# Second feed-forward product in one pass per column block: eleven groups in place of three lots, the last group in eight products

## The chip, the cores and the metric

The kernel runs on one core of one Trainium2 chip. The metric is the device time of one launch in microseconds (us). TensorE (PE) multiplies, VectorE (DVE) and ScalarE (ACT) work on tiles, GpSimd (POOL) and SyncE (SP) issue most of the transfers (DMAs).

## The reference

One encoder layer on x of 512 x 2048 (all float32): a root-mean-square norm, a wide input projection, an mLSTM in both directions and differential attention, two branch projections with gates, an output projection with residual, and then a gated feed-forward block and a last norm. The change is in the feed-forward block:

```python
h2 = _rmsnorm(x, norm2_w[l])
gate, up = jnp.split(h2 @ w_ffn_in[l], 2, axis=-1)     # D_FF = 5632
x = x + (jax.nn.silu(gate) * up) @ w_ffn_out[l]        # 5632 x 2048
...
return _rmsnorm(x, final_norm_w)
```

## The kernel before, in words

Every float32 product is made of three matmuls: each operand is split into a high part (a cast on ScalarE, L151) and a low part (a subtraction on VectorE, L152), and `mm3` (L145) adds high x high, low x high and high x low in PSUM.

The output projection (`wo_chunk`), the first feed-forward product (`fi_chunk`) and the second (`fo_chunk`) go through `seven` (L310), a Winograd form of Strassen's scheme: a group is 512 rows of the inner dimension, cut into 2 x 2 blocks, and seven block products (Q1 to Q7) take the place of eight. A column block is 1024 columns wide, two halves of 512. For all groups of a call the body runs three passes: Q1, Q5 and Q6 of every group; then Q2, Q3 and Q7 (the last group in another order); then Q4. Each product is 12 matmuls of 128 x 512 on the banks a, b or c (two PSUM tiles each). After the last group of a product, `post` evicts or adds the bank.

- *Right factors.* Per group six raw blocks a to f of 128 x 1024 (512 KB) come from memory by SP (`load`, L194), into 6 tiles `raw`. `t1_make` to `t4_make` form the sums on VectorE (t2 lives from the first pass to the third), and `parts` splits each of the seven factors into `whi` and `wlo`, three tiles each. `take` keeps two pieces ahead of the product, `issue` loads six raw blocks ahead.
- *Left factors.* For the second product they are the gated activations. The seven forms X11, S1, S2, X12, S3, S4, X22 of a group (128 x 512, 256 KB each) were written to memory by `turned` at the end of each `fi_chunk`. `loaded` (L438) brings them back by DMAs on POOL, and `factor` splits each into a high and a low tile, in the narrow tiles `x_` (32 of 128 x 512) or `t_` (39).
- *Lots.* All eleven groups' split factors do not fit in SBUF at once, so L834 cuts them into lots of 4, 4 and 3 groups. `lot_forms` loads and splits a lot's 28 (or 21) factors; it is called at Q2 of the chunk before, and its steps run one after each product through the list `behind` (`work`, L301). Each lot is used for both column blocks n = 0, 1: six chunks in all, in the order (lot 0, n 0), (lot 0, n 1), (lot 1, n 0) and so on.
- *Ends of chunks.* `added` (L649) evicts the banks. In lots 0 and 1 the eight output tiles of a chunk are added to `x1d` in memory by adding stores on POOL (L667). In the last lot the residual is fetched from `x1d` and added in SBUF, and `final` (L845) squares, scales and stores the rows.

Operations that are due later stand in a list with a program clock (`later`, `tick`). A scheduler then orders each engine's queue; within a queue everything runs in order.

## Time and profile before

| what | value |
|---|---|
| median of 3 runs | 2753.08 us (2750.37 to 2759.2) |
| the profiled execution's own time | 2750.09 us |
| its span, first to last instruction | 2748.3 us |
| mean granted TensorE clock | 0.988 |
| busy: PE, DVE, ACT, POOL | 2665.9, 1883.0, 1186.9, 194.3 us |
| moved by DMA | 435.59 MB, mean 158 GB/s |

Busy time is a sum over stages with different limits. PEclk is the share of full speed at which TensorE's clock was granted in a stretch. A DMA share of 1 means that all 16 transfer engines were busy. A matmul's shown length holds its pipeline; the distance between the starts of two is what it costs. In the rows, fi is the first feed-forward product, fo the second, fs a left factor on its way to fo, wo the output projection, and a name's L number is a line of the kernel.

### The profile page before, as it was taken

The numbers are of one execution on the slowest core, as the hardware profiler recorded it, in microseconds if no ns is written. First come the engines' busy times: TensorE is split into PE (matmuls) and PEld (weight loads), VectorE is DVE, ScalarE is ACT, GpSimd is POOL, SyncE is SP. The second block draws the span as 40 slices with busy tenths as digits, with TensorE's granted clock in tenths as the row PEclk, the third lists the DMA queues.
The fourth block names the chain that finished last, engine by engine and source line by source line (L and its number), as shares of the span: only waits on it lengthen the run. The fifth ranks groups of instructions, "written<-read, shape, count | busy, mean of one in ns | idle before, by whom it ended". The sixth has DMA issues, their size and how long they took to land.

```text
span 2748.3 us, 33249 instructions
## 1 busy us (share of the span) xinstructions
PE 2665.9 (97%) x12736; PEld 2227.7 (81%) x12736; DVE 1883.0 (69%) x2403; ACT 1186.9 (43%) x1641; POOL 194.3 (7%) x309
## 2 busy tenths in 40 slices
PE   7999999999999999999999999999999999898997
PEld 6888888888888888887778888888888878677776
DVE  5677776333444442487788888878888889686876
ACT  5444443222344432245464444444444455453544
POOL 2110100000000000001110000000000010111211
PEclk9999999999999999999999999999999999999999
DMA  5433332333322222347765555565555576677665
GB/s 194 125 105 95 81 104 97 111 112 111 100 92 93 92 92 92 127 151 215 242 193 185 189 176 180 175 208 188 182 184 191 197 253 194 213 214 214 209 201 162
DMA packets 138736, 435.59 MB, mean 158 GB/s; under 512 B 17848, under 2 KB 18408, under 8 KB 138576
## 3 DMA queue, kind: packets, MB, share of 16 engines
q1 hardware_dynamic: 103680, 353.56, 38.3%
q0 software_dynamic: 25056, 63.38, 9.1%
q10 hardware_dynamic: 9840, 16.52, 1.9%
q8 instruction: 100, 1.64, 0.2%
q14 instruction: 60, 0.49, 0.1%
HBM read 378.06 MB, written 44.84 MB: 154 GB/s over the span
## 4 chain that ended last, share of the span: by engine, by line
PE 61%; DVE 12%; issue 12%; DMA 11%; POOL 1%; ACT 1%; SPq 0%; ACTq 0%; DVEq 0%; POOLq 0%
PE fi_b L147 8%; PE ga_b L147 6%; PE gm_b L147 6%; PE aqk_b L147 6%; PE fi_a L147 6%; PE fi_c L147 6%; PE mqk_b L147 3%; PE mo_b L147 3%; PE ba_b L147 3%; PE mv_p L147 3%; DVE wlo_fi_Q L152 3%; PE av_p L147 3%; PE bm_b L147 2%; DVE wlo_fo_Q L152 2%; DMA raw_fo_b<-in_w_ffo 2%
## 5 line engine op out<-in xcount | busy, mean ns | idle before, releaser
L151 ACT CAST whi_fi_Q<-fi_Q_t 128x1024 fp32r<-128x1024 f32 x88 | 92.6, 1052 | 117.5 <-PE fi_b L147 95.5
L147 PE MATMUL aqk_b<-xh,whi_aqk 128*128 128x512 f32 x256 | 102.6, 404 | 11.9 <-ACT whi_aqk L151 7.8
L152 DVE TENSOR_TENSOR wlo_fi_Q<-fi_Q_t,whi_fi_Q 128x1024 fp32r<-128x1024 f32 x88 | 106.3, 1219 | 2.4 <-ACT whi_fi_Q L151 2.4
L147 PE MATMUL aqk_b<-xl,whi_aqk 128*128 128x512 f32 x256 | 102.2, 399 | 1.0 <-DVE xl L551 1.0
L333 DVE TENSOR_TENSOR raw_fi_e<-raw_fi_e,raw_fi_f 128x1024 f32<-128x1024 f32 x44 | 53.9, 1225 | 70.7 <-DMA raw_fi_e<-in_w_ffi 70.4
L147 PE MATMUL aqk_b<-xh,wlo_aqk 128*128 128x512 f32 x256 | 101.9, 398 | 0.3 <-DVE wlo_aqk L152 0.3
L147 PE MATMUL ga_b<-xh,whi_ga 128*128 128x512 f32 x256 | 100.0, 390 | 0.0
L147 PE MATMUL gm_b<-xh,whi_gm 128*128 128x512 f32 x256 | 99.7, 389 | 0.0
L147 PE MATMUL ga_b<-xl,whi_ga 128*128 128x512 f32 x256 | 99.7, 389 | 0.0
L147 PE MATMUL ga_b<-xh,wlo_ga 128*128 128x512 f32 x256 | 99.6, 389 | 0.0
L147 PE MATMUL gm_b<-xl,whi_gm 128*128 128x512 f32 x256 | 99.6, 389 | 0.0
L147 PE MATMUL gm_b<-xh,wlo_gm 128*128 128x512 f32 x256 | 99.6, 389 | 0.0
L152 DVE TENSOR_TENSOR wlo_gm<-raw_gm,whi_gm 128x1024 fp32r<-128x1024 f32 x32 | 39.2, 1225 | 84.4 <-ACT whi_gm L151 84.3
L320 DVE TENSOR_TENSOR raw_fi_b<-raw_fi_b,raw_fi_a 128x1024 f32<-128x1024 f32 x44 | 53.9, 1224 | 50.9 <-DMA raw_fi_b<-in_w_ffi 48.3
L151 ACT CAST whi_ga<-raw_ga 128x1024 fp32r<-128x1024 f32 x32 | 33.7, 1053 | 115.1 <-PE ga_b L147 62.4
L152 DVE TENSOR_TENSOR wlo_ga<-raw_ga,whi_ga 128x1024 fp32r<-128x1024 f32 x32 | 39.1, 1223 | 57.2 <-ACT whi_ga L151 57.2
L151 ACT CAST whi_gm<-raw_gm 128x1024 fp32r<-128x1024 f32 x32 | 33.7, 1053 | 103.1 <-PE gm_b L147 70.6
L151 ACT CAST whi_fi_Q<-raw_fi_e 128x1024 fp32r<-128x1024 f32 x44 | 46.4, 1055 | 70.7 <-PE fi_b L147 49.9
L151 ACT CAST whi_fi_Q<-raw_fi_b 128x1024 fp32r<-128x1024 f32 x44 | 46.6, 1058 | 67.0 <-PE fi_c L147 51.1
L151 ACT CAST whi_fi_Q<-raw_fi_f 128x1024 fp32r<-128x1024 f32 x44 | 46.5, 1056 | 64.1 <-PE fi_c L147 61.5
L147 PE MATMUL av_p<-whi_av,xh 128*128 128x256 f32 x256 | 72.9, 285 | 0.8 <-ACT whi_av L151 0.8
L147 PE MATMUL mv_p<-whi_mv,xh 128*128 128x256 f32 (+1 forms) x256 | 73.6, 287 | 0.0
(541 smaller groups left out, 8841.8 us busy)
## 6 DMA issues: line engine op xcount, KB each, us to landing
raw_fi_a<-in_w_ffi SPq DMA_DIRECT2D x44, 512.0 KB, 3.9
raw_fi_b<-in_w_ffi SPq DMA_DIRECT2D x44, 512.0 KB, 4.5
raw_fi_c<-in_w_ffi SPq DMA_DIRECT2D x44, 512.0 KB, 4.5
raw_fi_d<-in_w_ffi SPq DMA_DIRECT2D x44, 512.0 KB, 4.4
raw_fi_f<-in_w_ffi SPq DMA_DIRECT2D x44, 512.0 KB, 4.2
raw_fi_e<-in_w_ffi SPq DMA_DIRECT2D x44, 512.0 KB, 4.4
raw_ga<-in_w_ga SPq DMA_DIRECT2D x32, 512.0 KB, 3.5
raw_gm<-in_w_gm SPq DMA_DIRECT2D x32, 512.0 KB, 3.5
```

Source lines behind the costliest of these rows:

```text
L147: T.matmul(dst, lhs[l], rhs[r], start=first and i == 0, stop=last and i == 2, skip_group_check=skip)
L151: A.copy(hi, src)
L152: V.tensor_tensor(lo, src, hi.bitcast(F32), ALU.subtract)
L320: V.tensor_tensor(raws[r12], raws[r12], raws[r11], ALU.add)
L333: V.tensor_tensor(raws[r12], raws[r12], raws[r22], ALU.add)
```

## The change

- One pass per column block: `fo_chunk(n)` runs all groups, twice in all in place of six chunks. The adding stores to `x1d` go; the residual is fetched once per column block.
- No left factor stays. `stream()` lists, for both column blocks, every form in the order in which the products need it (74 per column block). Each is fetched four steps ahead by POOL, split where it is due, one step after each product, and kept until its product has used it. So each of them is loaded and split twice.
- The first ten groups use the seven products; the eleventh is computed plainly with eight (W12, W22, W11, W21, each times two left blocks), between the second and the third pass, on a fourth pair of banks d. Its forms S1 to S4 are not formed.
- `x_` becomes 16 tiles of 128 x 1024, which hold the high and the low part of one factor. In the second product these tiles take t2 and every second raw block, and eight raw blocks are loaded ahead instead of six.
- In `added`, the end of a tile whose residual is fetched by DMA is put 8000 ns of the program clock later, for the output projection too; the transposes behind it come 2000 after the end in all cases.

```diff
-    xpool = ctx.enter_context(tc.tile_pool(name="xpool", bufs=32))
+    xpool = ctx.enter_context(tc.tile_pool(name="xpool", bufs=16))
...
-        return xpool.tile([P, 512], dt, tag="x", name=name)
+        return xpool.tile([P, 1024], dt, tag="x", name=name)
...
-            name, src = sources[len(raws)]
-            raw = wpool.tile([P, src.shape[-1]], F32, tag="raw", name=f"raw_{name}", bufs=6)
+            name, src, x = sources[len(raws)]
+            raw = (x_(f"raw_{name}") if x else
+                   wpool.tile([P, src.shape[-1]], F32, tag="raw", name=f"raw_{name}", bufs=6))
...
-            load(need + 6)
+            load(need + (8 if sources[need][2] is not None else 6))
...
-    def seven(name, src, order, forms, post, start=None):
+    def seven(name, src, order, forms, post, start=None, plain=None, spare=False):
...
-            return source(f"{name}_{n}{g}", src(g, half, lot))
+            return source(f"{name}_{n}{g}", src(g, half, lot),
+                          len(sources) % 2 == 1 if spare else None)
...
-                t2[g] = ppool.tile([P, 1024], F32, tag="p", name=f"{nm}_t2")
+                t2[g] = (x_(f"{nm}_t2") if spare else
+                         ppool.tile([P, 1024], F32, tag="p", name=f"{nm}_t2"))
...
+        if plain is not None:
+            for n, at, to, posts in (
+                    ("W12", (0, 1), [("c", "X11"), ("d", "X21")], []),
+                    ("W22", (1, 1), [("c", "X12"), ("d", "X22")], ["D", "Q3"]),
+                    ("W11", (0, 0), [("a", "X11"), ("b", "X21")], []),
+                    ("W21", (1, 0), [("a", "X12"), ("b", "X22")], ["Q2"])):
+                r = raw(plain, *at, n)
+                add(n, plain, r, held(lambda r=r: raws[r]), to, posts)
...
+                for b_, f_ in to:
+                    if b_ not in bank:
+                        bank[b_] = [ps(f"{nm}_{b_}{i}") for i in range(2)]
+                    while f_ not in forms(g):
+                        work(True)
+                    hi, lo = forms(g)[f_]
...
+                    if b_ != to[-1][0]:
+                        work()
...
-    def factor(name, g, n, out, f_, src):
-        w = [slots(g, n + i)(f"{name}_{f_}{'hl'[i]}", F32R).rearrange("p (k c) -> p k c", k=2)
-             for i in range(2)]
+    def factor(name, n, out, f_, src):
+
+        if n < 16:
+            w = x_(f"{name}_{f_}", F32R)
+            w = [w[:, :512], w[:, 512:]]
+        else:
+            w = [t_(f"{name}_{f_}{i}", F32R) for i in "hl"]
+        w = tuple(x.rearrange("p (k c) -> p k c", k=2) for x in w)
         split(src, *w)
...
-            if final:
-                final(t, c, x[q, i])
-            else:
-                G.dma_start(x1d[t][c], x[q, i], accum_op=ALU.add)
+            final(t, c, x[q, i])
...
-                    end(22, i)
+                        later(8000, lambda i=i: end(22, i))
+                elif q_ == "D":
+                    V.tensor_tensor(x[22, i], x[22, i], bank["d"][i], ALU.add)
+                    fetch(22, i)
+                    later(8000, lambda i=i: end(22, i))
                 elif q_ == "Q3":
                     V.tensor_tensor(x[12, i], x[12, i], c_[i], ALU.add)
-                    if final:
-                        fetch(12, i)
-                    end(12, i)
+                    fetch(12, i)
+                    later(8000, lambda i=i: end(12, i))
...
-                later(9000 if c % 2 else 2000, lambda: turned(f"h2{c}", pair, 0, h2X[c], i,
+                later(2000, lambda: turned(f"h2{c}", pair, 0, h2X[c], i,
...
-            if q_ == "Q2" and j == NFB - 1:
-                lot_forms(0)
+            if q_ == "Q4" and j == NFB - 1:
+                stream()
...
-    LOTS = [range(0, 4), range(4, 8), range(8, NFB)]
+    GR = range(NFB - 1)
+
+    def stream():
+        need = [(g, f_) for g in GR for f_ in ("X11", "S1", "S2")]
+        need += [(g, f_) for g in GR[:-1] for f_ in ("X12", "S4", "S3")]
+        need += [(GR[-1], f_) for f_ in ("S3", "S4", "X12")]
+        need += [(NFB - 1, f_) for f_ in ("X11", "X21", "X12", "X22")]
+        need += [(g, "X22") for g in GR]
+        need = [(n, *gf) for n in range(2) for gf in need]
+        got = {}
+
+        def fetch(n):
+            if n < len(need):
+                _, g, f_ = need[n]
+                got[n] = half(f"fs{g}_{f_}")
+                G.dma_start(got[n], fgd[g][f_].rearrange("p (k c) -> p k c", k=2))
+
+        def make(n):
+            fetch(n + 4)
+            m, g, f_ = need[n]
+            factor(f"fs{m}_{g}", 16, fgf[m, g], f_, got.pop(n))
+
+        for n in range(4):
+            fetch(n)
+        for m, g, _ in need:
+            fgf[m, g] = {}
+        when(lambda: True, [lambda n=n: make(n) for n in range(len(need))])
...
-        seven(f"fo{m}_{n}", lambda g, h_, l: a["w_ffo"][n, g, h_, l], lot, lambda g: fgf[g],
-              added(f"fo{m}_{n}", n, *((lambda t, c: x1d[t][c], final) if last else ())), start)
+        seven(f"fo{n}", lambda g, h_, l: a["w_ffo"][n, g, h_, l], GR, lambda g: fgf[n, g],
+              added(f"fo{n}", n, lambda t, c: x1d[t][c], final, True), start, NFB - 1, True)
...
-    for m in range(len(LOTS)):
-        for n in range(2):
-            fo_chunk(m, n)
+    for n in range(2):
+        fo_chunk(n)
```

The first place is POOL's queue. Before, at the end of the first chunk (lot 0, n 0), where the last loads of lot 0 are followed by that chunk's adding stores:

```order
L446 DMA fs3_S4_18681<-fg3_S4d_157 128x512
L446 DMA fs3_X22_18683<-fg3_X22d_158 128x512
L667 DMA x1d2_1_109<-fo0_0_x220_18801 128x512
L667 DMA x1d3_1_113<-fo0_0_x221_18807 128x512
L667 DMA x1d0_1_101<-fo0_0_x120_18803 128x512
L667 DMA x1d1_1_105<-fo0_0_x121_18809 128x512
L667 DMA x1d0_0_100<-fo0_0_x110_19093 128x512
L667 DMA x1d1_0_104<-fo0_0_x111_19096 128x512
L667 DMA x1d2_0_108<-fo0_0_x210_18805 128x512
L667 DMA x1d3_0_112<-fo0_0_x211_18811 128x512
L446 DMA fs4_X11_19422<-fg4_X11d_159 128x512
```

In the changed kernel, where the first column block goes from its first pass to the second:

```order
L867 DMA fs9_S1_18950<-fg9_S1d_196 128x512
L867 DMA fs9_S2_18976<-fg9_S2d_195 128x512
L867 DMA fs0_X12_19000<-fg0_X12d_134 128x512
L867 DMA fs0_S4_19025<-fg0_S4d_136 128x512
L867 DMA fs0_S3_19051<-fg0_S3d_135 128x512
L867 DMA fs1_X12_19075<-fg1_X12d_141 128x512
L867 DMA fs1_S4_19100<-fg1_S4d_143 128x512
L681 DMA fo0_x210_19130<-x1d2_0_108 128x512
L867 DMA fs1_S3_19140<-fg1_S3d_142 128x512
L681 DMA fo0_x211_19137<-x1d3_0_112 128x512
```

The eight adding stores in a row are gone; loads of single factors follow one another in the order of use, with residual fetches (fo0_x) between them.

The second place is VectorE's queue. Before, in the second chunk (lot 0, n 1), second pass, where the factors of lot 1 (fs4 to fs7) are split beside the chunk's own weights:

```order
L152 TENSOR_TENSOR wlo_fo0_1_Q72_19580<-raw_fo0_1_e2_19428,whi_fo0_1_Q72_19579 128x1024
L152 TENSOR_TENSOR fs6_S1l_19627<-fs6_S1_19523,fs6_S1h_19626 128x512
L152 TENSOR_TENSOR fs7_X11l_19682<-fs7_X11_19595,fs7_X11h_19681 128x512
L152 TENSOR_TENSOR fs4_X12l_19760<-fs4_X12_19673,fs4_X12h_19759 128x512
L152 TENSOR_TENSOR wlo_fo0_1_Q73_19611<-raw_fo0_1_e3_19480,whi_fo0_1_Q73_19610 128x1024
L152 TENSOR_TENSOR fs7_S1l_19706<-fs7_S1_19597,fs7_S1h_19705 128x512
L152 TENSOR_TENSOR fs4_S3l_19780<-fs4_S3_19675,fs4_S3h_19779 128x512
L152 TENSOR_TENSOR wlo_fo0_1_Q33_19631<-raw_fo0_1_f3_19457,whi_fo0_1_Q33_19630 128x1024
```

In the changed kernel, first column block, first pass, groups 3 to 5:

```order
L152 TENSOR_TENSOR wlo_fo0_Q53_18635<-raw_fo0_b3_18415,whi_fo0_Q53_18634 128x1024
L152 TENSOR_TENSOR fs0_4_X11l_18653<-fs4_X11_18550,fs0_4_X11h_18652 128x512
L331 TENSOR_TENSOR fo0_Q66_t2_18883<-raw_fo0_b6_18656,raw_fo0_c6_18682 128x1024
L152 TENSOR_TENSOR wlo_fo0_Q63_18661<-fo0_Q63_t2_18658,whi_fo0_Q63_18660 128x1024
L152 TENSOR_TENSOR fs0_4_S1l_18679<-fs4_S1_18575,fs0_4_S1h_18678 128x512
L152 TENSOR_TENSOR wlo_fo0_Q14_18685<-raw_fo0_a4_18465,whi_fo0_Q14_18684 128x1024
L152 TENSOR_TENSOR fs0_4_S2l_18703<-fs4_S2_18601,fs0_4_S2h_18702 128x512
L323 TENSOR_TENSOR raw_fo0_b7_18731<-raw_fo0_b7_18731,raw_fo0_a7_18706 128x1024
L152 TENSOR_TENSOR wlo_fo0_Q54_18710<-raw_fo0_b4_18490,whi_fo0_Q54_18709 128x1024
```

One weight split and one factor split now alternate, the factor three products ahead of its use, and the sums of raw blocks stand two to three groups ahead.

The third place is ScalarE's queue at the end of the output projection's first column block. Before, with the squares x1j of rows whose residual a DMA brings:

```order
L151 CAST whi_wo0_Q41_10901<-wo0_Q61_t2_10483 128x1024
L748 ACTIVATE x1j2_1_10868,ss2p_116<-wo0_x220_10619 128x512
L748 ACTIVATE x1j3_1_10873,ss2p_116<-wo0_x221_10626 128x512
L151 CAST whi_wo0_Q42_10925<-wo0_Q62_t2_10544 128x1024
L748 ACTIVATE x1j0_1_10894,ss2p_116<-wo0_x120_10621 128x512
L748 ACTIVATE x1j1_1_10899,ss2p_116<-wo0_x121_10628 128x512
L748 ACTIVATE x1j0_0_10919,ss2p_116<-wo0_x110_10653 128x512
L748 ACTIVATE x1j1_0_10923,ss2p_116<-wo0_x111_10656 128x512
```

And in the changed kernel:

```order
L151 CAST whi_wo0_Q41_10854<-wo0_Q61_t2_10448 128x1024
L151 CAST whi_wo0_Q42_10878<-wo0_Q62_t2_10509 128x1024
L764 ACTIVATE x1j0_0_10872,ss2p_116<-wo0_x110_10618 128x512
L764 ACTIVATE x1j1_0_10876,ss2p_116<-wo0_x111_10621 128x512
L151 CAST whi_wo0_Q43_10912<-wo0_Q63_t2_10566 128x1024
```

The last cast (Q43), which stood behind six squares and a group of scaled transposes, now stands behind two squares, and these read rows whose residual was loaded long before.

## Rows read from the trace of the kernel before

**Rows 1.** The page, busy time and share of the span of each engine.
```profile
PE 2665.9 (97%) x12736; PEld 2227.7 (81%) x12736; DVE 1883.0 (69%) x2403; ACT 1186.9 (43%) x1641; POOL 194.3 (7%) x309
```
**Rows 2.** Windows: stretch, length, busy by engine, PEclk, DMA share, GB/s.
```profile
core 0: us, PE busy (x) PEld busy (x) DVE busy (x) ACT busy (x) POOL busy (x), PEclk, DMA share, GB/s
1800.00:2000.00 200.00, 199.86 (x899) 165.35 (x898) 163.06 (x166) 89.04 (x96) 0.00 (x0) 1.00 0.56 189
2263.00:2339.50 76.50, 75.62 (x337) 62.12 (x336) 67.73 (x74) 40.26 (x50) 5.28 (x6) 1.00 0.67 201
2339.50:2432.00 92.50, 83.39 (x343) 67.25 (x343) 66.65 (x70) 40.17 (x51) 19.49 (x31) 0.94 0.70 210
```
**Rows 3.** Timeline of TensorE (start, length): chunk starts, second product, last matmul.
```profile
2263.13 0.39 PE L147 MATMUL fo_a<-whi_fo_Q,fs_X11h 128*128 128x512 f32 x1
...
2265.85 0.39 PE L147 MATMUL fo_c<-whi_fo_Q,fs_S1h 128*128 128x512 f32 x1
...
2341.60 0.39 PE L147 MATMUL fo_a<-whi_fo_Q,fs_X11h 128*128 128x512 f32 x1
...
2435.38 0.56 PE L147 MATMUL fo_a<-whi_fo_Q,fs_X11h 128*128 128x512 f32 x1 [2.39 <-ACT whi_fo_Q L151]
...
2517.62 0.39 PE L147 MATMUL fo_a<-whi_fo_Q,fs_X11h 128*128 128x512 f32 x1
...
2609.76 0.39 PE L147 MATMUL fo_a<-whi_fo_Q,fs_X11h 128*128 128x512 f32 x1
...
2675.40 0.39 PE L147 MATMUL fo_a<-whi_fo_Q,fs_X11h 128*128 128x512 f32 x1
...
2735.88 0.39 PE L147 MATMUL fo_b<-whi_fo_Q,fs_X22l 128*128 128x512 f32 x1
```
**Rows 4.** Waits of TensorE from 2263 us on: total us, times, longest.
```profile
PE fo_a L147 <- DVE wlo_fo_Q L152: 18.7, 8, 4.0
PE fo_b L147 <- DVE wlo_fo_Q L152: 5.6, 3, 3.7
PE fo_c L147 <- DVE wlo_fo_Q L152: 4.8, 2, 2.6
```
**Rows 5.** Waits of VectorE from 2263 us on.
```profile
DVE raw_fo_b L320 <- DMA raw_fo_b<-in_w_ffo: 36.6, 12, 7.3
```
**Rows 6.** Timeline around 2335 us: POOL, SP and VectorE.
```profile
2330.60 3.49 POOL L667 DMA_DIRECT2D x1d<-fo_x  x4 [2.85 <-DVE fo_x L689]
...
2334.33 0.33 SPq L198 DMA_DIRECT2D raw_fo_b<-in_w_ffo  x1
...
2343.23 1.23 DVE L320 TENSOR_TENSOR raw_fo_b<-raw_fo_b,raw_fo_a 128x1024 f32<-128x1024 f32 x1 [6.65 <-DMA raw_fo_b<-in_w_ffo]
```
**Rows 7.** DMA issues from 2263 us on: count, size, median us to landing.
```profile
x1d<-fo_x POOLq DMA_DIRECT2D x32, 256.0 KB, 6.5
fo_x<-x1d POOLq DMA_DIRECT2D x16, 256.0 KB, 5.5
...
fs_S<-fg_S2d POOLq DMA_DIRECT2D x7, 256.0 KB, 8.7
```
**Rows 8.** Timeline of VectorE, back to back in the third chunk.
```profile
2450.25 1.22 DVE L152 TENSOR_TENSOR wlo_fo_Q<-fo_Q_t,whi_fo_Q 128x1024 fp32r<-128x1024 f32 x1
2451.39 0.69 DVE L152 TENSOR_TENSOR fs_X22l<-fs_X,fs_X22h 128x512 fp32r<-128x512 f32 x1
2451.99 1.22 DVE L152 TENSOR_TENSOR wlo_fo_Q<-raw_fo_a,whi_fo_Q 128x1024 fp32r<-128x1024 f32 x1
```
**Rows 9.** Timeline of TensorE in the first product's last block.
```profile
2217.23 0.80 PE L147 MATMUL fi_a<-wlo_fi_Q,h_X12h 128*128 128x512 f32 x1 [2.38 <-DVE wlo_fi_Q L152]
```
**Rows 10.** Timeline of ScalarE and TensorE at the output projection's first column block.
```profile
1289.79 0.63 ACT L748 ACTIVATE x1j<-wo_x 128x512 f32<-128x512 f32 x1 [3.81 <-DMA wo_x<-in_x]
...
1296.47 0.51 PE L147 MATMUL wo_b<-whi_wo_Q,mix_X22h 128*128 128x512 f32 x1 [1.78 <-ACT whi_wo_Q L151]
```
**Rows 11.** Windows with the columns of rows 2, beside bursts of factor loads.
```profile
2355.00:2360.00 5.00, 3.43 (x16) 2.50 (x14) 1.80 (x2) 2.09 (x2) 1.09 (x2) 1.00 1.03 405
...
2430.00:2445.00 15.00, 11.91 (x40) 8.97 (x39) 10.01 (x12) 7.30 (x11) 5.05 (x8) 0.77 1.05 358
```

More of the change, by code (lines that the diff above doesn't have):

```diff
@@ L345, in held, with add @@
             return lambda nm: parts(nm, get(), 2)
-        def add(q_, g, need, make):
+        def add(q_, g, need, make, to=None, posts=None):
             piece(f"{name}_{q_}{g}", need, make)
-            seq.append((q_, g))
+            to = to or [(BANK[q_], LEFT[q_])]
+            if posts is None:
+                posts = [q_] if g == order[-1] else []
+            seq.append((q_, g, to, posts))
         for g in order:
@@ L371, in body @@
             bank = {k: [ps(f"{nm}_{k}{i}") for i in range(2)] for k in "abc"}
-            for q_, g in seq:
+            last = {b_: n for n, (_, _, to, _) in enumerate(seq) for b_, _ in to}
+            begun = set()
+            for n, (q_, g, to, posts) in enumerate(seq):
                 if start and g == order[0]:
@@ L375, in body @@
                 w = take(it)
-                while LEFT[q_] not in forms(g):
-                    work(True)
-                hi, lo = forms(g)[LEFT[q_]]
-                for k in range(2):
-                    for i in range(2):
-                        sl = slice(i * P, (i + 1) * P)
-                        mm3(bank[BANK[q_]][i], [hi[:, k, sl], lo[:, k, sl]],
-                            [w[0][:, k], w[1][:, k]],
-                            q_ in ("Q1", "Q6", "Q5") and g == order[0] and k == 0,
-                            g == order[-1] and k == 1, skip=True)
-                    yield 6 * MM
-                if g == order[-1]:
+                for b_, f_ in to:
[4 more added lines that the diff above has]
+                    hi, lo = forms(g)[f_]
+                    for k in range(2):
+                        for i in range(2):
+                            sl = slice(i * P, (i + 1) * P)
+                            mm3(bank[b_][i], [hi[:, k, sl], lo[:, k, sl]],
+                                [w[0][:, k], w[1][:, k]], b_ not in begun and k == 0,
+                                n == last[b_] and k == 1, skip=True)
+                        yield 6 * MM
+                    begun.add(b_)
+                    if b_ != to[-1][0]:
+                        work()
+                for q_ in posts:
                     post(q_, bank)
@@ L446, in load_ @@
                     G.dma_start(X[f_], src[f_].rearrange("p (k c) -> p k c", k=2))
-            return load_, [lambda f_=f_, k=n + 2 * i: factor(name, g, k, out, f_, X.pop(f_))
+            return load_, [lambda f_=f_, k=7 * g + n + i: factor(name, k, out, f_, X.pop(f_))
                            for i, f_ in enumerate(fs)]
-        return two(0, ("X11", "S1", "S2")), two(6, ("X12", "S3", "S4", "X22"))
+        return two(0, ("X11", "S1", "S2")), two(3, ("X12", "S3", "S4", "X22"))
     def ahead(steps):
@@ L721, in turned @@
                     A.activation(out[f_][:, k], tv[:, k], AF.Copy, scale=scale(kk))
-            if keep and f_ != "X21":
+            if keep and f_ in keep:
                 nc.scalar.dma_start(keep[f_].rearrange("p (k c) -> p k c", k=2), out[f_])
-        if keep and len(out) == 4:
+        if keep and "S1" in keep and len(out) == 4:
             def sum_(f_, to, l, r, op):
@@ L779, in rstd2 @@
         env["r"], env["r2"] = r, r2
-    fgd = [spilled(f"fg{j}") for j in range(NFB)]
+    fgd = [spilled(f"fg{j}") for j in range(NFB - 1)]
+    fgd.append(spilled(f"fg{NFB - 1}", ("X11", "X12", "X21", "X22")))
     def fi_chunk(j):
@@ L867, in start @@
         def start(q_):
-            if q_ == "Q2" and n == 1 and not last:
-                lot_forms(m + 1)
-            if q_ == "Q1" and n == 0 and last:
+            if q_ == "Q4" and n == 0:
                 env["fnw"] = [t_(f"fnw{c}") for c in range(4)]
```

63 lines of the change are left out of this document (25 added, 38 removed).

## The prediction

> **What bounds the kernel now.** I read the busy times first, then busy time by stretch, then the timeline of TensorE, then who waited for whom, and last the DMA side. TensorE is busy 97% of the span, VectorE 69% and ScalarE 43% [rows 1]. In a stretch of the first feed-forward product TensorE is busy 199.86 of 200 us: there nothing but its own work counts. In the second product it is not so: between 2339.5 and 2432 us it is busy 83.39 of 92.5 us, at a granted clock of 0.94 [rows 2]. So the second product is the stage to price.
>
> One product is 12 matmuls; the first of one and the first of the next stand at 2263.13 and 2265.85, so a product costs 2.72 us [rows 3]. The six chunks of the second product begin at the further times of [rows 3] and the last matmul starts at 2735.88 and takes 0.23, so they last 78.5, 93.8, 82.2, 92.1, 65.6 and 60.7 us. Their 28, 28, 28, 28, 21 and 21 products need 76.2 (four times) and 57.1 us (twice). The chunks therefore lose 2.3, 17.6, 6.1, 16.0, 8.5 and 3.6 us, together 54.1; about 0.9 of it is eight transposes of the first product's last block, so **53.2 us are lost**.
>
> The list of waits says to what: TensorE waited 18.7, 5.6 and 4.8 us for the split of the right factor on VectorE [rows 4]; much of the rest is slower matmuls after such stops (a clock of 0.94 over 92.5 us is 5.5 us [rows 2]). VectorE in turn waited 36.6 us for the raw blocks b of the right factor alone, up to 7.3 at a time [rows 5]. One case in full: SP issues a block b at 2334.33, POOL issues the adding stores of a finished lot from 2330.60, and VectorE begins its sum with b at 2343.23, after 6.65 us of waiting [rows 6]. The two chunks that lose 17.6 and 16.0 us are the second and the fourth: each begins with the adding stores of the chunk before and holds nine factor loads in a row, and 28 factor splits for the next lot. The clean references are the first chunk (2.3 less 0.9 = 1.4 us) and the last (3.6 us, with its fetches of the residual).
>
> **The change, term by term.** The sum stands against the profiled execution, 2750.1 us (span 2748.3); the median of the runs, 2753.1, is 3.0 above it.
>
> *Products.* Before 11 groups x 7 x 2 = 154; now (10 x 7 + 8) x 2 = 156. Two more at 2.72 us on the engine that bounds: **+5.4 us**.
>
> *Lots.* Four of six chunk ends go, with 32 adding stores (median 6.5 us to land [rows 7]) and with 10 VectorE and 8 ScalarE operations each. The 16 residual fetches stay (5.5 us [rows 7]). The bursts of nine loads go as well; factors now come one per product.
>
> *Factors.* Splits rise from 77 to 148. On VectorE a weight split starts 1.14 us before what follows it, a factor split 0.60 us [rows 8]. A group of the first pass has three weight splits and two sums (5 x 1.14) and three factor splits (3 x 0.60): 7.5 us of VectorE beside 8.16 us of TensorE, 92%. The second pass is the same, the third 1.74 of 2.72. Over the stage: 71 more factor splits (+43 us), 6 fewer weight splits and 8 fewer sums (-16 us), 36 fewer evictions at 0.60 (-22 us). VectorE's total hardly moves; it is spread evenly instead of in heaps. ScalarE, 40.26 of 76.5 us in the first chunk [rows 2], takes one cast more per product and stays far from full. This work is covered as long as VectorE is not made to wait.
>
> *Raw blocks.* Every second one goes to the 16 wide tiles that the left factors no longer use there, so up to a dozen are ahead instead of six. That cover matters: in the case above VectorE got its block 8.9 us after the issue [rows 6], over three products.
>
> *What TensorE still loses.* The nearest rows are the chunks that load no factors, 1.4 and 3.6 us, and those with bursts and a full VectorE, 17.6 and 16.0 us [rows 3]. Below: 2 x 1.4 = 3 us. Above: 2 x 16 = 32 us. I take 10, near the lower end: per column block 3.6 for the same residual fetches and 1.4 for a VectorE that is full to 92%. So 53.2 becomes 10: **-43.2 us**. If the cover of early raw blocks were missing, the upper end would hold.
>
> *Last block of the first product.* Its second half carries the 28 factor splits of lot 0 today, and TensorE waits up to 2.38 us there [rows 9]. Now four factors come in its last pass. **-2.5 us**, from 0 to -5 (the wait again for the slow matmuls behind it).
>
> *End of the output projection.* ScalarE's squares wait for a fetch (3.81 us idle) ahead of the last splits in its queue, and TensorE waits 1.78 us for such a split [rows 10]; the second column block has the twin. With most squares behind the last split these waits go. What is late next is the transposes' own input. **-5 us**, from 0 (that is as late) to -8 (start-up and clock included).
>
> *Others, at nothing.* The wide tiles hold high and low part together with the same bytes, and each part is waited for alone. At the program's start two x loads move behind two weight loads on SP; TensorE has other column blocks to fill in with, and I put it at 0, plus or minus 2 us. The tail behind the last matmul, 2748.3 - 2736.1 = 12.2 us, is the same code.
>
> Sum: 5.4 - 43.2 - 2.5 - 5 = -45.3, so 2704.8 us against 2750.1; with the offset of 3.0, **2708 us** as a median. With the good ends (3, -5, -8) it is 2750.1 + 5.4 - 50.2 - 13 + 3 = 2695 us. A measurement here tells about 0.3%, 8.3 us, from no change.
>
> **Rivals.**
>
> *A, the forecast, 0.70.*
>
> *B, VectorE has no slack, 0.16.* At 92% any late block passes straight to TensorE, and the two column blocks each lose what the heaped chunks lose: 32 us in place of 10, with no gain at the output projection. 2750.1 + 5.4 - 21.2 - 2.5 + 3 = 2735 us, 2724 to 2750. For it: nearly all waits of TensorE in this stage end with VectorE's split [rows 4]. Against: they came when VectorE stood still for memory [rows 5], not when it worked.
>
> *C, the transfers bound, slower, 0.07.* Place: the first two passes, 40 times three products. Each needs three raw blocks of 512 KB and three factors of 256 KB, 2.36 MB in 8.16 us, 289 GB/s, where the stage moves 201 to 210 now [rows 2]. The forecast's gain is eaten when each of the 40 takes 45.3 / 40 = 1.13 us longer, that is below 254 GB/s; at 240 GB/s it is 9.83 us, 40 x 1.67 = 67 us more, 2775 us. Against: 405 GB/s over 5 us and 358 over 15 us with these very loads in flight [rows 11].
> The Trainium skill, "DMA: Bandwidth & Descriptors", section Bandwidth, asks for transfers of at least 1 MiB (341 GB/s at 1 MB, 138 at 64 KB); at 256 KB an estimate between the two may fall under 254. By that rule the 71 added loads would make C the case; the trace disagrees as long as several loads are in flight.
>
> *D, POOL's queue, 0.04.* The program fetches a factor four products before its split, 10.9 us. Now they land in 8.7 us at the worst median [rows 7]. If they took longer than 10.9 us, each of 148 would cost a quarter of the landing less 2.72: at 12 us 0.28 x 148 = 41 us, no gain; at 14 us 115 us, slower. It decides from 12 us on. Against: the 8.7 us are from bursts of nine, which go.
> The Trainium skill, "SBUF — State Buffer", section "SBUF: two separate sides" (its box on the "DVE blocks DMA" trap), says that loads issued by GpSimd starve for descriptors while VectorE runs an operation in a 2-port mode. By that rule D would be the case if the fp32 subtracts were such operations; the loads of [rows 7] landed beside them, and no run here shows the lock itself.
>
> *E, little happens, 0.03.* The stalls move to other places: 2745 to 2760 us.
>
> **How the numbers follow.** Faster by over 0.3%: A, most of B and a bit of D, 0.70 + 0.14 + 0.01 = 0.85. Same: the rest of B, E and a bit of D, 0.02 + 0.03 + 0.01 = 0.06. Slower: C and half of D, 0.07 + 0.02 = 0.09. The likeliest case gives 2708 us. The range leaves out no more than 2 in 10: C, D and E (0.14) and the upper end of B; its low end lies 2 us under the sum of the good ends: 2693 to 2738 us.
>
> **What would show it.** Right: two column blocks of 78 x 2.72 = 212 us of products with some 5 us lost in each; the granted clock near 1.00 in them; VectorE's waits for raw blocks far under 36 us; VectorE 85 to 90% busy; DMA at 260 to 290 GB/s. B would show many short waits of TensorE for splits, all along the passes. C would show VectorE waiting for raw blocks in every group and the DMA share near 1. D would show ScalarE's factor casts waiting for loads. The forecast is wrong if TensorE loses over 25 us in the two column blocks, or if the gain comes from ahead of 2180 us.

## The result, and the profile after

The changed kernel takes 2719.5 us (median of 4 runs, 2716.1 to 2722.0) against 2752.1 for the kernel before; the ratio is 0.988 (95% interval 0.986 to 0.990). The forecast was 2708 us, the range 2693 to 2738. The profiled execution has a span of 2719.9 us where before had 2748.3. By stage, from the starts of the first matmul of each in the two timelines:

| stage | before | after | forecast of the difference | measured |
|---|---|---|---|---|
| up to the output projection | 1215.6 | 1214.4 | 0 | -1.2 |
| output projection | 179.7 | 175.3 | -5 | -4.4 |
| first feed-forward product | 867.8 | 865.7 | -2.5 | -2.1 |
| second product | 473.0 | 454.0 | +5.4 - 43.2 = -37.8 | -19.0 |
| behind the last matmul | 12.2 | 10.5 | 0 | -1.7 |

So one term is wrong, by half. Each profile is one execution, and these stages differ a little between executions. The changed kernel and seven of the runs below share its output projection and, but for the last block, its first feed-forward product: there the way up to the output projection took 1214.4 to 1218.0 us, the output projection 173.7 to 177.7 and the first product 864.4 to 871.6. So the -4.4 is a real gain (with the code of before it took 179.7 and 178.7), while the -2.1 and the -1.2 lie within that spread. The timeline of TensorE has the start of either column block and the last matmul, beside [rows 3]:

```profile
2255.40 0.39 PE L147 MATMUL fo_a<-whi_fo_Q,fs_X11h 128*128 128x512 f32 x1
...
2485.27 0.39 PE L147 MATMUL fo_a<-whi_fo_Q,fs_X11h 128*128 128x512 f32 x1
...
2709.20 0.39 PE L147 MATMUL fo_b<-whi_fo_Q,fs_X22l 128*128 128x512 f32 x1
```

From 2255.40 to 2709.43 are 454.0 us; 156 products of 2.72 need 424.3. TensorE loses 29.7 us where the forecast said 10 (before 54.1, eight transposes included). Counted product by product (the time from one product's first matmul to the next less 2.72), 14.0 of it lies in the two second passes (9.3 and 4.7), 12.8 at the start of the two Q4 passes (5.7 and 7.1), and most of the rest (2.7) at the start of the stage. The windows, with the columns of [rows 2], show a second pass (second row) beside a first:

```profile
2263.00:2339.00 76.00, 75.54 (x337) 62.59 (x338) 71.72 (x78) 46.06 (x62) 13.36 (x25) 1.00 0.69 245
2340.00:2430.00 90.00, 83.90 (x358) 67.78 (x358) 76.78 (x88) 51.21 (x68) 20.45 (x38) 0.98 0.86 298
```

What TensorE waited for in the second product (total us, times, longest), beside [rows 4], and VectorE, beside [rows 5]:

```profile
PE fo_b L147 <- ACT whi_fo_Q L151: 5.1, 2, 3.5
PE fo_c L147 <- DVE wlo_fo_Q L152: 5.0, 4, 1.7
PE fo_b L147 <- DVE wlo_fo_Q L152: 4.4, 4, 1.9
PE fo_a L147 <- DVE wlo_fo_Q L152: 2.1, 3, 1.1
```
```profile
DVE wlo_fo_Q L152 <- ACT whi_fo_Q L151: 23.8, 19, 9.9
DVE raw_fo_e L337 <- DMA raw_fo_e<-in_w_ffo: 11.9, 9, 2.2
DVE raw_fo_b L323 <- DMA raw_fo_b<-in_w_ffo: 10.9, 4, 5.0
DVE raw_fo_e L337 <- DMA raw_fo_f<-in_w_ffo: 7.0, 3, 2.9
...
DVE raw_fo_e L337 <- issue: 3.8, 2, 2.1
DVE fo_Q_t L344 <- DMA raw_fo_d<-in_w_ffo: 2.1, 4, 0.7
```

TensorE's four rows add up to 16.6 us of the 29.7; the slow matmuls behind such stops (last section) are a part of the rest. VectorE's first row, waits for casts, belongs to the second loss below. In the other five VectorE still stands 35.7 us, 31.9 of them until a raw block lands and 3.8 ("issue") for nothing that the profile names, though up to a dozen blocks can be held. All five rows are of sums, none of a split. One case in the timelines of SP, ScalarE, VectorE and TensorE:

```profile
2351.83 0.33 SPq L199 DMA_DIRECT2D raw_fo_e<-in_w_ffo  x1
```
```profile
2357.28 1.06 ACT L151 CAST whi_fo_Q<-raw_fo_e 128x1024 fp32r<-128x1024 f32 x1 [1.15 <-PE fo_b L147]
```
```profile
2362.43 1.23 DVE L337 TENSOR_TENSOR raw_fo_e<-raw_fo_e,raw_fo_f 128x1024 f32<-128x1024 f32 x1 [2.23 <-DMA raw_fo_e<-in_w_ffo]
2363.57 1.22 DVE L152 TENSOR_TENSOR wlo_fo_Q<-raw_fo_e,whi_fo_Q 128x1024 fp32r<-128x1024 f32 x1
```
```profile
2364.84 0.50 PE L147 MATMUL fo_b<-wlo_fo_Q,fs_S3h 128*128 128x512 f32 x1 [1.93 <-DVE wlo_fo_Q L152]
```

TensorE wants the split of 2363.57. Which blocks these are is told by VectorE's order, where names have their group's number (wlo_fo0_Q72 is the low part of Q7 of group 2, raw_fo0_e5 block e of group 5):

```
2102 L337 TENSOR_TENSOR raw_fo0_e5_19376<-raw_fo0_e5_19376,raw_fo0_f5_19351 128x1024
2103 L152 TENSOR_TENSOR wlo_fo0_Q72_19355<-raw_fo0_e2_19146,whi_fo0_Q72_19354 128x1024
```

The sum of group 5 stands ahead of the split of group 2, nine products before it is due, and waits for a block that SP issued 10.6 us earlier. The split behind it had its input in SBUF since the sum of e2, and the cast that it also needs had ended at 2358.34. Nothing is late but the order. The case of [rows 6] in the kernel before is the same: the sum that waits 6.65 us is of group 2, and behind it stand the splits of a and b of group 0, the products that TensorE wants next:

```
2077 L320 TENSOR_TENSOR raw_fo0_1_b2_19149<-raw_fo0_1_b2_19149,raw_fo0_1_a2_19131 128x1024
2078 L152 TENSOR_TENSOR wlo_fo0_1_Q10_19134<-raw_fo0_1_a0_18941,whi_fo0_1_Q10_19133 128x1024
2079 L152 TENSOR_TENSOR wlo_fo0_1_Q50_19153<-raw_fo0_1_b0_18960,whi_fo0_1_Q50_19152 128x1024
```

The second loss is on ScalarE. Its squares (x2j, for the last norm) wait for the fetch of the residual (column block 0), or come six in a row with the norm behind them (column block 1), ahead of the casts of the Q4 pass; two rows of ScalarE and the two matmuls that waited:

```profile
2451.34 0.63 ACT L883 ACTIVATE x2j<-fo_x 128x512 f32<-128x512 f32 x1 [8.62 <-DMA fo_x<-x1d]
...
2685.94 2.94 ACT L151 CAST whi_fo_Q<-fo_Q_t 128x1024 fp32r<-128x1024 f32 x3 [0.41 <-ACT fo_x L900]
```
```profile
2456.83 0.49 PE L147 MATMUL fo_b<-whi_fo_Q,fs_X22h 128*128 128x512 f32 x1 [1.61 <-ACT whi_fo_Q L151]
...
2687.04 0.79 PE L147 MATMUL fo_b<-whi_fo_Q,fs_X22h 128*128 128x512 f32 x1 [3.54 <-ACT whi_fo_Q L151]
```

### The profile page after: what moved, and what is told of

The parts are those of the page before. It is cut to its first block, busy times and chain, and to the rows that moved or that the text cites. A ratio compares the mean times of both kernels' runs of the same rounds, so it can differ in the third digit from the quotient of the medians.

```text
span 2719.9 us, 33514 instructions
## 1 busy us (share of the span) xinstructions
PE 2659.3 (98%) x12760; PEld 2226.9 (82%) x12760; DVE 1887.9 (69%) x2420; ACT 1202.2 (44%) x1674; POOL 208.8 (8%) x348
## 5 line engine op out<-in xcount | busy, mean ns | idle before, releaser
L147 PE MATMUL aqk_b<-xs,whi_aqk 128*128 128x512 f32 x512 | 164.3, 399 | 12.8 <-ACT whi_aqk L151 7.2
L147 PE MATMUL ga_b<-xs,whi_ga 128*128 128x512 f32 x512 | 158.2, 390 | 0.0
L147 PE MATMUL gm_b<-xs,whi_gm 128*128 128x512 f32 x512 | 157.9, 389 | 0.0
L147 PE MATMUL fi_a<-whi_fi_Q,h_X 128*128 128x512 f32 x440 | 147.0, 391 | 0.0
L147 PE MATMUL fi_c<-whi_fi_Q,h_S 128*128 128x512 f32 x440 | 145.8, 392 | 0.0
L147 PE MATMUL fi_b<-whi_fi_Q,h_S 128*128 128x512 f32 x352 | 115.5, 389 | 0.0
L147 PE MATMUL aqk_b<-xs,wlo_aqk 128*128 128x512 f32 x256 | 101.6, 397 | 0.4 <-DVE wlo_aqk L152 0.3
L147 PE MATMUL ga_b<-xs,wlo_ga 128*128 128x512 f32 x256 | 99.6, 389 | 0.0
L147 PE MATMUL gm_b<-xs,wlo_gm 128*128 128x512 f32 x256 | 99.6, 389 | 0.0
L147 PE MATMUL mv_p<-whi_mv,xs 128*128 128x256 f32 (+1 forms) x512 | 98.3, 287 | 0.0
```

What stands on the lines that cost most here:

```text
L147: T.matmul(dst, lhs[l], rhs[r], start=first and i == 0, stop=last and i == 2, skip_group_check=skip)
```

## The experiments

Theory S: sums that the scheduler puts early on VectorE wait there for fresh blocks while due splits stand behind them. Theory W: squares do the same to casts on ScalarE. The rivals: T (the transfers are too slow), Q (POOL's queue) and P (the prediction's reading of the kernel before). "Lost" is the second product's time less its 154 or 156 products at 2.72 us, from each profile. The medians come from four comparisons, in which the kernel before took 2751.8 to 2753.9 us.

| run | median us | ratio to before (interval) | second product us | lost |
|---|---|---|---|---|
| before, changed | 2752.1, 2719.5 | 0.988 (0.986, 0.990) | 473.0, 454.0 | 54.1, 29.7 |
| e1_sums | 2717.0 | 0.987 (0.985, 0.989) | 445.5 | 21.1 |
| e2_late | 2711.0 | 0.985 (0.982, 0.987) | 439.6 | 15.3 |
| e3_fetch21 | 2722.6 | 0.989 (0.987, 0.991) | 452.5 | 28.2 |
| e5_six | 2729.1 | 0.991 (0.989, 0.994) | 456.9 | 32.5 |
| e4_half | 2710.5 | 0.985 (0.983, 0.986) | 437.6 | 13.3 |
| e7_both | 2695.5 | 0.979 (0.978, 0.981) | 425.5 | 1.2 |
| e9_before_sums | 2705.3 | 0.983 (0.982, 0.984) | 430.5 | 11.6 |
| e11_sums3 | 2699.7 | 0.982 (0.980, 0.984) | 432.0 | 7.7 |
| e8_wo | 2750.0 | 0.999 (0.998, 1.000) | 472.9 | 54.0 |
| e10_both_seven | 2694.5 | 0.979 (0.977, 0.981) | 424.1 | 5.2 |
| e13_all_stages | 2676.8 | 0.972 (0.971, 0.974) | 424.6 | 5.7 |
| e14_before_all | 2687.8 | 0.976 (0.975, 0.978) | 432.2 | 13.3 |

**e1_sums.** The four sums of `t1_make` to `t4_make`, in the second product alone, are tied behind what is written before them on VectorE:

```diff
+        pin = tc.keep_in_program_order if spare else (lambda ins: ins)
...
-                V.tensor_tensor(raws[r12], raws[r12], raws[r22], ALU.add)
+                pin(V.tensor_tensor(raws[r12], raws[r12], raws[r22], ALU.add))
```

> The changed kernel with one edit: the sums of right factors in the second product keep their written place on VectorE, directly ahead of their own split (now some stand up to three groups, nine products, ahead of splits that are due sooner). In the changed kernel the second passes of the two column blocks (products 31 to 60) lose 9.2 and 4.6 us of TensorE time, and VectorE waits 35.7 us for raw blocks. Theory S (an early sum waits for a block that was just issued, and ready splits stand behind it): those losses fall under 5 us together, VectorE's waits for raw blocks under 10 us, the span by 7 to 11 us, to about 2711. Rival T (the transfers are too slow, in whatever order they are used): the waits move to the splits and casts of the same blocks, the second passes still lose 11 us or more, span within 3 us of 2720. Rival Q (POOL stands for 27.6 us behind a fetch of the residual and then issues its loads in a heap): about half is left, 6 to 8 us, span about 2714.

VectorE's waits for raw blocks are gone, all of them, and the second passes lose 5.6 us in place of 14.0. What is left stands where a pass begins (2.1 and 2.5 us at products 32 and 110): now the sum is too late, behind the additions to the finished tiles. T falls: the waits did not move to the splits, and no cast of ScalarE waits for a block to land either. By its waits S holds; its number (under 5) was missed and 5.6 lies close to Q's 6 to 8, so that Q is decided by e3_fetch21. The span fell by 3.6 only: the Q4 pass of column block 1 lost 8.3 in place of 7.1, that of block 0 2.1 in place of 5.7, the first passes 5.1 in place of 2.9, and the stage began 4.9 us later in this execution.

**e2_late.** The finished tiles end one per product, and the squares keep their place on ScalarE:

```diff
-                    later(8000, lambda i=i: end(22, i))
+                    later(11000 + 2700 * i, lambda i=i: end(22, i))
...
+                    later(16400 + 2700 * i if plain else 8000, lambda i=i: end(12, i))
...
+                        later(11400 + 2700 * i, lambda i=i: end(11, i))
...
+            tc.keep_in_program_order(
+                A.activation(j, x, AF.Square, accum_out=ss3p[:, t * 4 + c:t * 4 + c + 1]))
```

> The changed kernel with one edit: the squares (and with them the norm) of the finished tiles in the second product are due later, one per product, and stay on ScalarE behind the casts written before them. In the changed kernel the Q4 passes of the two column blocks start with losses of 5.7 and 7.1 us. Theory W (the squares wait for the fetch of the residual, or fill ScalarE, ahead of casts that are due): both losses fall under 1.5 us, the span by 9 to 11 us, to about 2710. Rival (the work has nowhere to go): it moves behind the last matmul, the tail grows from 10.5 us by 4 or more and the span falls by 7 us or less.

The Q4 passes lose 0.7 and 0.0 us, the tail is 11.1, the span 2710.8. W holds.

**e3_fetch21.** The adding fetch of rows 2 and 3 moves from the post of Q1 to that of Q7:

```diff
-                    fetch(21, i)
+                    if not plain:
+                        fetch(21, i)
...
+                    if plain:
+                        tc.keep_in_program_order(fetch(21, i))
```

> The changed kernel with one edit: the fetch that adds the residual to the tiles of rows 2 and 3, first column, is issued at the end of the second pass instead of the end of the first, so POOL no longer stands 27.6 us at it while PE finishes the first pass. Theory Q (the heap of loads that POOL issues when it gets free delays the raw blocks): the losses right behind the turn from first to second pass (5.0 us in column block 0, products 31 to 40, and 1.4 in block 1) go, the span falls by 5 to 7 us, to about 2714. Theory S (early sums on VectorE are the cause, the heap only sets where it shows): these losses show up at other products of the second pass, whose sum stays within 3 us of 13.9; span 2717 to 2720.

The second passes lose 10.4 and 1.8, together 12.2: the loss has moved (3.7 at the 31st product, right at the turn, where it was 1.1; 4.7 at the 56th, where it was 0.8) and nearly kept its size. Q falls: POOL no longer stands still there, and the turn loses more, not less.

**e5_six.** The raw blocks are as before, six slots and six ahead:

```diff
-                          len(sources) % 2 == 1 if spare else None)
+                          None)
```

> The changed kernel with one edit: the raw blocks of the second product use only the six narrow slots and are loaded six ahead, as in the kernel before (t2 stays in the wide tiles). The prediction's claim (the dozen of blocks ahead is what covers the passes): TensorE's losses in the second product rise from 29.6 us to over 45, span 2736 or more. Theory S (the slots were used up by sums that stand early, a block is still first read 4 to 9 us after its issue): hardly a change, losses 26 to 36 us, span 2717 to 2727.

32.5 us are lost, 3 more than with the dozen of slots, by far not the 16 or more that the prediction's reading wants: 8.2 in the first passes (2.9 with the dozen), 10.9 in the second (14.0). By the medians six slots cost more, 9.6 us, so the dozen is worth something; what, one profile each does not show. In VectorE's order the sums of e now have two to six other splits of right factors between them and their own, one to two groups; with the dozen it was eight to fifteen, three groups and more. The scheduler had spent the added slots on sums that stand earlier still. So the cover never came about: counted from the timelines of SP and VectorE, half of the sums of e began within 4.6 us of the issue of their later block in the kernel before, within 5.1 in the changed one and within 4.7 here.

**e4_half.** Every second fetch of a factor is left out, so neighbouring factors are split from one tile:

```diff
+                if n % 2:
+                    got[n] = got[n - 1]
+                    return
```

> The changed kernel with every second fetch of a left factor left out (two neighbouring factors are split from the same loaded tile, so the second product's result is another): 74 loads of 256 KB in place of 148, all splits and products stay. Theory S (early sums): the raw blocks still are read right after they land, the second passes lose 9 to 14 us (14.0 with all loads), span 2714 to 2720. Rival T (the transfers of the two first passes are near their bound): the second passes lose 6 us or less, VectorE's waits for raw blocks fall from 35.7 us under 15, span 2711 or less.

This one is nearer to T than to S: the second passes lose 3.4 us (T: 6 or less, S: 9 to 14) and the span is 2711.9, though the waits at raw blocks fall to 22.7 only, not under 15. The sums stand as early as before; that blocks which land sooner make an early sum wait less is one reading of it. That the transfers are no bound of their own is shown by the next run, with all the loads.

**e7_both.** The squares of e2_late, and a tie for the sums: each must stand behind the third split ahead of its own, so that at most two others lie between (`lows` collects the split of each right factor):

```diff
+        def pin(ins):
+            if spare:
+                tc.add_manual_dep(ins.ins, lows[-3].ins.name, mybir.DependencyInfo(
+                    mybir.DependencyClass.NoSync, mybir.DependencyReason.DATA), reason="pin")
```

> The changed kernel with two edits together: the late squares of the run before, and the sums held back less strictly (a sum may stand on VectorE up to three splits ahead of its own, no further). Theory (sums that stand too early and squares that stand too early are two separate losses and add up): the second passes lose 4 us or less in place of 14.0, the Q4 passes 1 or less in place of 12.8, the start 3.5 stays; TensorE loses 8 us in the second product in place of 29.7, median about 2699 (2695 to 2704). Rival (a stall that goes brings TensorE sooner to the next wait): 14 us or more are left, median 2706 or more.

1.2 us are lost in 425.5, less than expected: the first pass lost 1.1, not 3.5, and nothing new came up. Now the blocks are early: half of the sums of e begin 24.9 us or more after the issue. Three windows, with the columns of [rows 2]:

```profile
2260.00:2335.00 75.00, 75.00 (x336) 61.94 (x336) 72.85 (x80) 45.02 (x59) 11.51 (x21) 1.00 0.80 286
2335.00:2430.00 95.00, 95.00 (x420) 78.62 (x419) 89.23 (x101) 59.86 (x81) 27.00 (x48) 1.00 0.91 314
2480.00:2560.00 80.00, 80.00 (x355) 66.20 (x354) 75.73 (x84) 48.94 (x65) 17.67 (x31) 1.00 0.80 280
```

TensorE is busy without a gap at full granted clock while VectorE is busy 89.23 of 95 us and the transfers run at 314 GB/s.

**e9_before_sums.** The same tie in the kernel before (for names that begin with fo), nothing else.

> The kernel before with one edit: in the second product a sum may stand on VectorE up to three splits ahead of its own, no further. Adding stores, the heaps of factor loads and the six slots stay. Theory S (early sums are also the cause of the 53.2 us that the six chunks lose): VectorE's waits for raw blocks fall under 10 us, the chunks lose under 35 us, the median falls by 18 us or more, to 2734 or less. Rival P, the prediction's reading (blocks are late because of the adding stores and the heaps of nine loads): the waits move to the casts of the same blocks, the chunks lose 48 us or more, median within 6 us of the kernel before.

46.5 us, more than the whole change. The six chunks lose 1.6, 0.0, 0.7, 0.0, 4.6 and 4.7 us; the second and the fourth, which begin with adding stores and hold the heaps of nine loads, lose nothing. POOL's queue still has all the stores and, behind them, the nine loads in a row. The window of the second chunk, beside the last of [rows 2]:

```profile
2339.50:2432.00 92.50, 92.11 (x407) 75.95 (x406) 81.21 (x87) 50.78 (x65) 24.03 (x38) 1.00 0.87 273
```

VectorE's waits in the second product, beside [rows 5], before:

```profile
DVE raw_fo_e L333 <- DMA raw_fo_e<-in_w_ffo: 35.3, 17, 5.2
DVE wlo_fo_Q L152 <- ACT whi_fo_Q L151: 14.2, 20, 1.9
```

and with the tie:

```profile
DVE wlo_fo_Q L152 <- ACT whi_fo_Q L151: 45.6, 55, 3.1
...
DVE raw_fo_e L338 <- DMA raw_fo_e<-in_w_ffo: 1.4, 2, 0.8
```

Of 36.6 us for blocks b and 35.3 for blocks e 1.4 are left. VectorE waits for ScalarE's casts instead, as P said, but those do not wait for blocks (ScalarE waits with them 142.0 us for matmuls of TensorE and 25.7 for the sums), and TensorE hardly feels it. P falls: stores, heaps and six slots stay, and 42.5 of the 54.1 us go.

**e11_sums3.** The changed kernel with that tie alone.

> The changed kernel with the sums of the second product held to three splits ahead of their own, and nothing else; it stands beside the kernel before with the same one edit (2705.3 us, six chunks losing 11.6 us). Theory S (the early sums were the whole trouble of the passes in both kernels, and one pass over all groups gains nothing more there): the passes lose 2 us or less, the start of the Q4 passes still 12.8, so 14 us of loss and 5.4 us of added products against 11.6: median 2707 (2704 to 2711), no faster than the kernel before with that edit. Rival P, the prediction's (lots, adding stores and heaps cost something of their own): median 2699 or less.

The median, 2699.7, meets neither number. It is nearer to P's, but its five runs lie between 2698.6 and 2706.7, those of e9_before_sums between 2703.9 and 2708.4, and the intervals of the two ratios overlap: no difference between the two kernels with the tie is shown. In the profiled executions the second product takes 432.0 us, in the kernel before with the tie 430.5: one pass gains nothing there, 5.4 us of added products against 3.9 less of loss. What lies between the two executions comes from ahead of it: the output projection takes 176.2 (178.7), a gain of the change that I had left out of the expectation, and the first product 864.4 (870.1), which is within its spread. The Q4 pass of column block 0 lost 0.9, not 5.7; why is not known.

**e8_wo.** The change's edit of the output projection in the kernel before:

```diff
-                    end(22, i)
+                    if nm[:2] == "wo":
+                        later(8000, lambda i=i: end(22, i))
+                    else:
+                        end(22, i)
...
-                later(9000 if c % 2 else 2000, lambda: turned(f"h2{c}", pair, 0, h2X[c], i,
+                later(2000, lambda: turned(f"h2{c}", pair, 0, h2X[c], i,
```

> The kernel before with the change's edit of the output projection alone (the end of the Q7 and Q3 tiles due 8 us later, all turned activations due 2 us after). Prediction: TensorE starts the first feed-forward product 5 us sooner (0 to 8), and nothing else moves: median 2747. Rival (the 5.6 us by which the changed kernel starts that product sooner come from elsewhere, the start-up or chance): within 2 us of the kernel before.

-1.9 us by the medians, within the rival's 2, and an interval of the ratio that holds 1; -2.1 in the stage (177.6 for 179.7). So the edit alone is not shown to gain anything. Its 177.6 is one execution and lies at the edge of the 173.7 to 177.7 of the changed kernel's stage, so it does not show either that the rest of the 4.4 us has another source.

**e10_both_seven.** e7_both with the eleventh group like the others (`GR = range(NFB)`, no plain products, seven forms kept).

> The run with both edits (2695.5 us, 1.2 us of loss), and the last group in seven products like the others: 154 products in place of 156, 74 factor splits per column block become 77, the last group's seven forms are written and read again. Theory (TensorE alone bounds the second product now, a product is 2.72 us): 5.4 us less, median 2690 (2688 to 2693). Rival (the last group's sums of activations are late for the second pass, or the extra factors are): 3 us less or nothing, median 2692 or more.

The rival's number holds: 1.0 us by the medians. The second product is 1.4 us shorter, not 5.4, since it loses 5.2 us where e7_both lost 1.2 (2.9 in a first pass, 2.3 in a Q4 pass). The first product takes 869.8 us for 865.3, which is within its spread; in its last block TensorE waits 3.75 us for one split, 1.1 in e7_both.

**e13_all_stages.** e10_both_seven with the tie in all three seven-product stages (`if len(lows) >= 3` in place of `if spare`).

> The run before this one (both edits, seven products for each group) with the sums held to three splits ahead in the output projection and the first feed-forward product as well. In the changed kernel VectorE waits 25.9 us for raw blocks in the output projection, where TensorE loses about 13 us between 1285 and 1396, and over 100 us in the first product, where TensorE loses nothing. Theory S: the first feed-forward product starts 5 to 9 us sooner after the start of the output projection (now 175.3 us), the first product stays at 866 us, median 2683 (2680 to 2687). Rival (the output projection waits for its activations, squares and transposes, not for raw blocks; and held sums come too late where VectorE has slack): within 3 us of the run before, or slower.

2676.8 us, 77 below the kernel before in the same comparison. The output projection takes 164.2 us (176.3), the first product 859.2 (869.8), more than expected, and both lie under every execution without the tie in that stage. There too the sums stood early: from 1214 to 2240 us the changed kernel's VectorE waited 24.0 us for blocks b and e of the output projection and 102.0 for those of the first product, and now it waits for none.

**e14_before_all.** That tie in the kernel before, as its only edit.

> The kernel before with one edit: in all three seven-product stages (output projection, first and second feed-forward product) a sum may stand on VectorE up to three splits ahead of its own, no further. Six chunks, 154 products, adding stores, heaps of loads and immediate squares stay. Theory S (early sums were the loss, wherever the stage): 2705.3 us (held in the second product alone) less about 12 in the output projection and 10 in the first product, median 2683 (2679 to 2690), within 14 us of the best version so far (2676.8), so that the change itself accounts for 14 us or less of the 75 between it and the kernel before. Rival (the early stages gained because the changed kernel also moved squares and activations there): 2693 us or more.

2687.8 us: 66 us below before in the same comparison, 32 below the changed kernel. The output projection takes 172.5, the first product 859.9. S holds, and all that e13_all_stages has beside the tie is worth 11 us (2676.8).

## Why the prediction was right in size and wrong in its reason

- **Products, +5.4.** Right as a price: 156 at 2.72 us are 424.3, and e7_both runs them in 425.5. To take the two out again gained 1.4 us of the stage only (e10_both_seven).
- **Last block of the first product, -2.5; output projection, -5; start-up, 0.** Measured -2.1, -4.4 and -1.2. Only the second is clear of the spread between executions, and its reason is not shown: the edit alone gave 1.9 us, with an interval that holds no change.
- **The tail, 0.** -1.7; what shortened it was not looked into.
- **What TensorE still loses, 53.2 to 10.** This step failed: 29.7, and by the prediction's own sign (over 25 us lost) the forecast was wrong, although the time fell in the range. Its account of before was that blocks came late for three reasons, the adding stores, the heaps of loads and the six slots, and that the change takes all three away. e9_before_sums leaves all three in place and loses 11.6: what cost the time was the order on VectorE, sums ahead of due splits. The reason was in the rows that I read: [rows 6] has VectorE idle in a sum, and I asked why its block was late, not whose block it was and what stood behind it. The prediction also calls VectorE full in the second chunk; by [rows 2] it was busy 66.65 of 92.5 us there, and 67.73 of 76.5 in the first, which lost little. And the changed kernel's order showed sums two to three groups ahead, which got no price. That the time came out near the forecast is in part luck: the early sums cost 42.5 us before (54.1 less 11.6) and 22.0 after (29.7 less 7.7), and no run shows why the change halved them.
- **Raw blocks, "that cover matters".** Not in this way: with six slots 32.5 us are lost, with twelve 29.7 (9.6 us apart by the medians). First use followed issue as closely as before (4.6 and 5.1 us for half of the sums of e), since sums were put as early as slots allowed; and with the tie six slots are enough for waits of 1.4 us (e9_before_sums). The sentence that without the cover the upper end (32) would hold came out nearly to the number, because the cover was used up.
- **The same residual fetches cost 3.6 per column block.** The Q4 passes, where they end, lost 5.7 and 7.1. ScalarE's squares stood just ahead of ten casts that are due one per product, and with later squares (e2_late) the loss is 0.7 and 0.0. I had counted the edit of `later` for the output projection alone; that it moved these squares is likely, but no run takes it back by itself.
- **Rivals.** The outcome lies between A (2708) and B (2735). B's mechanism falls: at 89.23 of 95 us VectorE holds TensorE up nowhere in e7_both. C falls with the same window: 314 GB/s, nothing lost, which e4_half alone would not have shown. D's place, POOL, stood still for 27.6 us behind an adding fetch, and without that (e3_fetch21) the second passes lost 12.2 in place of 14.0. E's time, 2745 to 2760, is excluded.
- **The other signs.** They fit in part. The two column blocks:

```profile
2255.00:2485.00 230.00, 219.69 (x946) 178.08 (x945) 196.32 (x221) 127.21 (x174) 49.51 (x87) 0.99 0.76 255
2485.00:2709.40 224.40, 217.72 (x938) 176.85 (x937) 177.24 (x200) 121.18 (x165) 41.02 (x71) 0.98 0.59 193
```

The clock was near 1.00 as forecast, VectorE busy 85 and 79% (forecast 85 to 90), the transfers at 255 and 193 GB/s (260 to 290). VectorE's waits at raw blocks, 35.7 us, were not far under 36.

The Trainium skill, "PSUM — Partial Sum Buffer", section "Engine vs sequencer instructions", says that the queues of ScalarE, VectorE and GpSimd are strictly first in, first out. The rows above agree: 2.23 us idle at a sum with a ready split behind it.

**Open:** what shortened the output projection; why early sums cost half as much in two column blocks as in six chunks; and the 8.4 us by which the start of the second product moves between executions that are alike up to the last block of the first product (2255.3 to 2263.7).

## What to carry to other kernels

When an in-order engine waits for a transfer, look first at what stands behind the waiting instruction: an operation that is not due for nine products must not stand ahead of one that is due now. A scheduler may put it there, and twelve slots in place of six were room to put it earlier still. (Why this scheduler did so, whether it takes transfers to be shorter than they are, was not looked into.) Tie such operations to within a few steps of their use (three splits here; the written place itself was too late at the turn of a pass), and only then judge the larger structure: here one tie in the kernel before gave 66 us, the restructuring without it 33, and restructuring, later squares and tie together 77.

## What the runs showed of the hardware that was not expected

With 148 loads of 256 KB and 128 of 512 KB in the second product, transfers ran at 314 GB/s over 95 us at a DMA share of 0.91, beside a VectorE busy 94% of the time, and TensorE lost nothing (e7_both). The loads of factors that POOL issued there landed in 3.8 to 7.6 us (medians by tile), below the 10.9 us of four products by which they are fetched ahead.

A short wait cost more than its own time here. In the changed kernel TensorE stood for 1.93 us at 2364.84; the windows from there on have its granted clock (the column PEclk of [rows 2]) at 0.67 and 0.57, means of stretches at 2.4 and at 1.2 GHz, where it was 1.00 ahead of the wait:

```profile
2362.50:2364.90 2.40, 0.47 (x3) 0.06 (x1) 2.40 (x3) 2.08 (x3) 0.00 (x0) 1.00 0.52 200
2364.90:2367.50 2.60, 2.60 (x8) 2.08 (x9) 2.60 (x3) 0.00 (x0) 0.55 (x1) 0.67 0.62 197
2367.50:2369.50 2.00, 2.00 (x6) 1.55 (x6) 2.00 (x4) 0.34 (x1) 0.55 (x1) 0.57 0.71 215
```

That product took 6.40 us (2362.52 to 2368.92) in place of 2.72: 3.7 for a wait of 1.9.
